# Expert weights in rows of 8 KB: whole gate and up rows into four PSUM banks, down rows in neighbouring pairs

## The chip, the core and the metric

The kernel runs on one core of a Trainium2 chip. The metric is the device time of one execution in microseconds. It is the median of three runs; a separate execution was profiled, and its trace is what the views below show.

## What is computed

The reference is one layer of an encoder with 512 tokens of width 1024: three token mixers (differential attention, attention in a window, attention to 256 memory tokens) whose outputs are gated, summed and projected, then a mixture of 16 experts, then a last norm. The change touches the experts. Each expert picks its 64 best tokens (`cap` below), and every weight is used once, in float32:

```python
def expert_choice_ffn(h, w_router, w_gate, w_up, w_down):
    ...
    cap = max(1, EC_FACTOR * s // N_EXPERTS)
    logits = jnp.einsum('bsd,de->bse', h, w_router).astype(jnp.float32)
    aff = jax.nn.softmax(logits, axis=-1)
    g, idx = lax.top_k(jnp.swapaxes(aff, 1, 2), cap)
    bidx = jnp.arange(b)[:, None, None]
    xe = h[bidx, idx]
    a = jnp.einsum('becd,edf->becf', xe, w_gate)
    u = jnp.einsum('becd,edf->becf', xe, w_up)
    ye = jnp.einsum('becf,efd->becd', jax.nn.silu(a) * u, w_down)
    ye = ye * g[..., None].astype(ye.dtype)
    return jnp.zeros_like(h).at[bidx, idx].add(ye)
```

`w_gate` and `w_up` are 16 matrices of 1024 x 2048, `w_down` 16 of 2048 x 1024, all stored row by row. That is 24 MB for an expert.

## The kernel before

The dense part comes first: norms, projections, the three mixers, the output projection and the router. It takes a little less than half of the span, and its weights come in slabs of 1 MB on SP's queue (lines 85 to 94). The change leaves it alone. Its last lines give, for every token and expert, the affinity (`aff`) and the place among the expert's 64 (`slot`). While its tensor engine is idle, line 610 issues products that nobody reads (`keep_clock`).

The experts run two at a time, eight pairs (line 730). The even expert of a pair has partitions 0 to 63 of its results, the odd one 64 to 127, and the two products of a step lie in different halves of the tensor engine's columns. A pair goes like this:

- `onehots` (line 679) makes 0/1 matrices from the places. `gather` (line 733) multiplies them with the tokens `x2` on the tensor engine (line 738), which picks and transposes the tokens at once; the result is `xT`. `picked_rstd` picks the tokens' norm factors `rp` (line 693).
- Gate and up: for each of four column groups of 512 (`fc`, line 757) there is one PSUM bank for gate and one for up. `half_up` loads two slabs, one for each expert, with four k steps of 128 rows by 512 columns: on each partition four rows of 2 KB (`load_up`, line 698). `mult_up` multiplies them (line 705). Two halves complete a bank.
- After each group ACT makes Silu of the gate bank (line 770), DVE multiplies with up (line 771), the tensor engine transposes the 512 columns in four pieces (line 774), and ACT puts them into `hT` (line 775), the left side of the down product.
- Down: each slab has two blocks of 128 rows of `w_down`, on each partition two rows of 4 KB that lie 128 rows apart (line 784). `down` multiplies into two banks `y` (line 716).
- `scatter` (line 719) copies a bank out of PSUM, multiplies with the transposed affinities (line 723) and adds the result to the tokens' sums `acc` (line 725).

A float32 product appears in the trace as two matmul records, so a k step of both experts into one bank is four of them.

The last pair has a down part of its own (lines 806 to 822): column groups of 512, 256 and 256, whose rows are 2 KB and 1 KB, so that little is left to do when the last weights arrive. The final norm and the output follow.

PSUM has eight banks here: two each named `tr`, `y`, `gate` and `up` (`ps_e`, line 647).

What sets the order of the loads is `slot_e` (line 660). The slabs of the experts go through a fixed list of 1 MB buffers. The first 22 places (`order`) become free one by one in the dense part, and three kinds of buffer among them are used once only: half of `hx`, the two halves of `acc` and `low`. From then on the 18 buffers in `slots` take turns. All loads are issued on SP's queue, which is worked off in order: a load whose buffer is still being read stops the loads behind it. The first four loads that wait for a buffer are issued in halves (line 667), so that each half waits for half of the old slab's products only.

In pair 0 the tensor engine starts on three pairs of slabs in a fixed order (`in_order`) before the second half of the gather is issued (lines 747 to 756). Elsewhere a planner orders the instructions of each engine.

Of the kernel before, what the change touches and what calls it, by code (L numbers as in the profile page):

```python
# [8 lines left out]
F32 = mybir.dt.float32  # L9
# [39 lines left out]
def trunk_kernel(ctx, tc, x, mem, attn_norm_g, mem_norm_g, w_in, w_mem_kv, lq1, lk1, lq2, lk2,  # L49
# [45 lines left out]

# [1 line left out]
    ident = const.tile([P, P], F32, name="ident")  # L97
# [11 lines left out]
    def rstd_of(ss, n, width, tmp):  # L109
        """1 / sqrt(ss / width + EPS), with a Newton step."""  # L110
        s = tmp.tile([P, n], F32, name="rs_s")
        r = tmp.tile([P, n], F32, name="rs_r")
        t = tmp.tile([P, n], F32, name="rs_t")
        u = tmp.tile([P, n], F32, name="rs_u")
        ACT.activation(s, ss, AF.Sqrt, bias=eps, scale=1.0 / width)
        DVE.tensor_scalar(u, ss, -0.5 / width, -0.5 * EPS, op0=OP.mult, op1=OP.add)
        DVE.reciprocal(r, s)
        DVE.tensor_mul(t, r, r)
        DVE.tensor_mul(t, t, u)
        DVE.scalar_tensor_tensor(r, t, 1.5, r, OP.add, OP.mult)  # L120
        return r
# [31 lines left out]
    def proj_n(slab, ah, al, acc, t_outer=False, low=None):  # L153
        """acc[t]: where the tokens of tile t go; two of them may share a bank."""
        nt = len(acc)
        ws = []

        def part(t, k):
            if k // 4 == len(ws):
                ws.append(split_w(slab[:, k // 4 * 4:k // 4 * 4 + 4, :], 4, 256, low))  # L160
            wh, wl = ws[k // 4]
            (o, first, last), a = acc[t], slice(t * P, (t + 1) * P)
            PE.matmul(o, ah[:, k, a], wh[:, k % 4, :], start=(k == 0 and first), stop=False, skip_group_check=True)  # L163
            PE.matmul(o, ah[:, k, a], wl[:, k % 4, :], start=False, stop=False, skip_group_check=True)  # L164
            PE.matmul(o, al[:, k, a], wh[:, k % 4, :], start=False, stop=(k == KT - 1 and last),  # L165
                      skip_group_check=True)

        if t_outer:
            for t in range(nt):
                for k in range(KT):  # L170
                    part(t, k)
                yield t
        else:
            for k in range(KT):
                for t in range(nt):
                    part(t, k)
# [9 lines left out]
    def norm_t(src, nt, g, hi, lo, tmp, gb=None, between=None):  # L186
        """Normalised tokens, transposed and split; the gain on the rows (gb) or on the columns (g)."""
        for t in range(nt):
# [40 lines left out]
    def project(w_o, merged, first=False, spare={}, slabs=range(4)):  # L229
        """spare: a third place for split weights, while two wait for the last heads."""  # L230
        for s in slabs:
# [13 lines left out]

# [1 line left out]
    with ExitStack() as as_:  # L247
# [124 lines left out]

# [1 line left out]
    with ExitStack() as bs:  # L374
# [76 lines left out]

# [1 line left out]
    with ExitStack() as cs:  # L453
# [81 lines left out]

# [1 line left out]
    m_hi = hpool.tile([P, KT, S], F32R, name="m2_hi", tag="h_hi", bufs=1)  # L537
# [55 lines left out]

# [1 line left out]
    aff = ep.tile([P, TT, N_EXP], F32, name="aff")  # L595
# [9 lines left out]
    def keep_clock(n, after, w=512):  # L605
        """Products that nobody reads: an idle tensor engine falls to half its clock."""
        with tc.issue_after(after.ins):
            ps = ps_pj()
            for _ in range(n):
                PE.matmul(ps[:, :w], ident, x2[:, 0, :w], start=True, stop=True)  # L610
# [32 lines left out]

# [1 line left out]
    pse = pool(ctx, "pse", space=PSUM)  # L645
# [6 lines left out]
    hx = hpool.tile([P, 2, 2048], F32, name="hx", tag="h_lo", bufs=1)  # L652
    hT = hx[:, 0].rearrange("p (f c) -> p f c", c=P)
    low, high = (etmp[:, 4 * i:4 * i + 4, :].rearrange("p a b -> p (a b)") for i in range(2))
# [9 lines left out]

    def slab_e(parts, src):
        """A slab of weights; the first ones that wait for a slot come in halves, which are free sooner."""
        n = 1 + (0 <= count[0] - len(order) < 4)
        v = slot_e().rearrange("p (k c) -> p k c", k=parts)
        for i in range(n):
            ks = slice(i * parts // n, (i + 1) * parts // n)  # L670
            nc.sync.dma_start(v[:, ks], src(ks.start, ks.stop - ks.start))
        return v
# [24 lines left out]

    def load_up(w, pr, fc, half):
        return [slab_e(4, lambda k, n, i=i: dap(w, (2 * pr + i) * D * DE + (4 * half + k) * P * DE + fc * 512,
                                                (DE, P), (P * DE, n), (1, 512))) for i in range(2)]  # L700

    def mult_up(sl, half, ps, todo, in_order=False):
        for k4, i in todo:
            k = 4 * half + k4
            mm = PE.matmul(ps[i * 64:(i + 1) * 64], xT[:, k, i * 64:(i + 1) * 64], sl[i][:, k4, :],  # L705
                           start=(k == 0), stop=(k == KT - 1))
            if in_order:
                tc.keep_in_program_order(mm)
        return mm

    def half_up(w, pr, fc, half, ps):
        mult_up(load_up(w, pr, fc, half), half, ps, [(k4, i) for k4 in range(4) for i in range(2)])

# [5 lines left out]
    def scatter(y, ys, n, w, squares=None):  # L719
        (ACT.copy if n else DVE.tensor_copy)(ys[:, :w], y[:, :w])  # L720
        for t in range(TT):
            ps = ps_e(("tr", "tr", "gate", "up")[t] if squares else "tr")[:, :w]
            PE.matmul(ps, gt[:, t * P:(t + 1) * P], ys[:, :w], start=True, stop=True)  # L723
# [6 lines left out]
    for pr in range(N_EXP // 2):  # L730
# [12 lines left out]
        if pr:  # L743
            gather(0)
            gather(4)
            rp = picked_rstd()
        if not pr:
            gather(0, 2)
            gather(2, 2)
            pgs, pus = [ps_e("gate") for _ in range(2)], [ps_e("up") for _ in range(2)]  # L750
            for w, fc, ps in ((w_exp_gate, 0, pgs), (w_exp_up, 0, pus), (w_exp_gate, 1, pgs)):
                mm = mult_up(load_up(w, 0, fc, 0), 0, ps[fc], [(k4, i) for i in range(2) for k4 in range(4)], True)
            behind = mm.ins
            with tc.issue_after(behind):
                gather(4)
                rp = picked_rstd()
        for fc in range(DE // 512):
            if not pr and fc < 2:
                pg, pu = pgs[fc], pus[fc]
            else:  # L760
                pg, pu = ps_e("gate"), ps_e("up")
            with tc.issue_after(behind):
                if pr or fc > 1:
                    half_up(w_exp_gate, pr, fc, 0, pg)
                half_up(w_exp_gate, pr, fc, 1, pg)
                if pr or fc:
                    half_up(w_exp_up, pr, fc, 0, pu)
                half_up(w_exp_up, pr, fc, 1, pu)
            act = ep.tile([P, 512], F32, name="esq", bufs=1)
            silu = ACT.activation(act, pg, AF.Silu, scale=rp)  # L770
            DVE.scalar_tensor_tensor(act, pu, rp, act, OP.mult, OP.mult)  # L771
            ps = ps_e("tr")
            for j in range(4):
                PE.transpose(ps[:, j * P:(j + 1) * P], act[:, j * P:(j + 1) * P], ident)  # L774
            ACT.activation(hT[:, 4 * fc:4 * fc + 4, :], ps.rearrange("p (k c) -> p k c", k=4), AF.Copy)  # L775
# [4 lines left out]

        if pr < N_EXP // 2 - 1:
            y = [ps_e("y") for _ in range(2)]
            for f2 in range(DE // 256):
                sl = [slab_e(2, lambda k, n, i=i: dap(w_exp_down, (2 * pr + i) * DE * D + (2 * f2 + k) * P * D,
                                                      (D, P), (P * D, n), (1, D))) for i in range(2)]
                for j in range(2):
# [5 lines left out]

        # the last norm's gain, from a column to every row
        ones, diag, gf = tmp_a[:, :P], tmp_a[:, 512:1024].rearrange("p (k c) -> p k c", k=4), tmp_a[:, 1024:]
        POOL.memset(ones, 1.0)
        for i, name in enumerate(("gate", "up")):
            ps = ps_e(name)
            DVE.tensor_mul(diag, ident[:, None, :].to_broadcast([P, 4, P]),
# [3 lines left out]

        # the last pair by columns, so that little is left when its last weights arrive
        with tc.issue_after(silu.ins):
# [18 lines left out]

# [1 line left out]
    c1 = 2  # L825
# [59 lines left out]
```

## Time and profile before

| | |
|---|---|
| median of three runs | 1820.2 us (1819.51 to 1820.83) |
| span of the profiled execution | 1817.1 us |
| tensor engine busy | 1706.3 us, 94% |
| mean granted clock of the tensor engine | 0.993 |
| bytes moved by DMA | 477.69 MB |
| HBM read | 468.94 MB, 259 GB/s over the span |

The span reaches from the first to the last instruction of the profiled execution; that and the runs' times are measured apart. "PE" is the tensor engine's matmul, "PEld" its weight load, "SPq" the queue of SP, which issues the loads. In the page's forty slices each digit is a busy share in tenths. "PEclk" is the granted clock. "DMA share" is the mean busy share of the core's 16 DMA engines; it can pass 1 since an engine's packets overlap. Windows give for a stretch the busy time of each engine with its number of instructions, then clock, DMA share and GB/s. The chain is the work that ended last, followed back from the end; a row has start, length, engine and line. KB in a row of DMA issues are 1024 bytes; GB/s count 10^9 bytes.

### The profile page before, as it was taken

The page shows a single profiled execution, that of the slowest core. Times are in us where ns is not written, and L with a number is a line of the kernel's source. Part 1 is how long each engine was busy: PE and PEld are TensorE (multiplying, and loading weights), DVE is VectorE, ACT ScalarE, POOL GpSimd, SP SyncE. Part 2 cuts the span into 40 slices and gives each one's busy share as a digit, 9 for nine tenths or more (in the row PEclk, how much of TensorE's full clock was granted, in tenths as well). Part 3 has the DMA queues.
Part 4 walks back from the last instruction along what each step waited for, and adds up shares of the span by engine and source line. Part 5 has one row for each costly group of instructions (what it writes and reads, how often), then busy time and mean ns, then how long its engine had stood idle before and what let it go on. Part 6 is the DMA issues. An engine that isn't in the chain of part 4 may idle for free.

```text
span 1817.1 us, 21484 instructions
## 1 busy us (share of the span) xinstructions
PE 1706.3 (94%) x8749; PEld 1046.6 (58%) x8749; DVE 523.4 (29%) x1057; ACT 456.0 (25%) x937; POOL 182.1 (10%) x165
## 2 busy tenths in 40 slices
PE   8999999999999999999999988988988988988987
PEld 7888888878879888974343332432422422422423
DVE  4388733464355444441020100100100200101003
ACT  4377752376534343320001000000000000000011
POOL 2043310164430001100000000000000000000000
PEclk9999999999999999999999999999999999999999
DMA  5442222412225226659999999999999999999997
GB/s 167 106 103 71 70 70 93 116 48 70 71 70 186 83 68 244 232 185 333 404 386 394 400 387 398 396 386 402 392 387 406 387 388 405 387 392 401 387 387 258
DMA packets 251557, 477.69 MB, mean 263 GB/s; under 512 B 8257, under 2 KB 84337, under 8 KB 251458
## 3 DMA queue, kind: packets, MB, share of 16 engines
q1 hardware_dynamic: 249506, 470.85, 70.9%
q0 software_dynamic: 1952, 5.47, 1.6%
q8 instruction: 69, 1.13, 0.3%
q14 instruction: 30, 0.25, 0.0%
HBM read 468.94 MB, written 2.10 MB: 259 GB/s over the span
## 4 chain that ended last, share of the span: by engine, by line
PE 73%; DMA 24%; DVE 1%; ACT 1%; SPq 1%; issue 0%; DVEq 0%; ACTq 0%
PE up L705 10%; PE gate L705 9%; PE pj L148 8%; PE pj L150 8%; PE pj L149 8%; DMA slot<-in_w_exp_down_dram 5%; DMA slot<-in_w_exp_up_dram 5%; PE y L716 4%; DMA slab<-in_w_exp_down_dram 4%; PE tr L723 3%; PE tr L738 3%; DMA sp<-in_w_exp_down_dram 2%; DMA etmp<-in_w_exp_down_dram 2%; PE pj L163 2%; PE pj L164 2%; PE pj L165 2%
## 5 line engine op out<-in xcount | busy, mean ns | idle before, releaser
L705 PE MATMUL up<-slot,sp 128*64 128x512 f32 x712 | 201.7, 600 | 23.7 <-DMA slot<-in_w_exp_up_dram 23.7
L716 PE MATMUL y<-slot,hx 128*64 128x512 f32 (+1 forms) x672 | 208.5, 582 | 14.7 <-DMA slot<-in_w_exp_down_dram 14.5
L705 PE MATMUL gate<-slot,sp 128*64 128x512 f32 x680 | 204.0, 597 | 4.8 <-DMA slot<-in_w_exp_gate_dram 4.8
L148 PE MATMUL pj<-h_hi,w 128*128 128x512 f32 x464 | 182.3, 393 | 0.2 <-DVE aks L139 0.2
L150 PE MATMUL pj<-h_hi,w 128*128 128x512 f32 x464 | 182.0, 392 | 0.0
L149 PE MATMUL pj<-h_lo,w 128*128 128x512 f32 x464 | 181.7, 392 | 0.0
L131 DVE TENSOR_TENSOR w<-slab,w 128x1024 fp32r<-128x1024 f32 x111 | 145.1, 1308 | 122.0 <-ACT w L130 121.8
L771 DVE SCALAR_TENSOR_TENSOR esq<-up,rpick,esq 128x512 f32<-128x512 f32 x32 | 24.0, 751 | 511.6 <-PE up L705 503.8
L130 ACT ACTIVATE w<-slab 128x1024 fp32r<-128x1024 f32 x113 | 119.0, 1055 | 119.7 <-PE pj L150 69.8
L705 PEld LDWEIGHTS up<-slot,sp 128*64 128x64 f32 x712 | 63.9, 138 | 116.6 <-issue 91.2
L716 PEld LDWEIGHTS y<-slot,hx 128*64 128x64 f32 x672 | 62.2, 136 | 113.4 <-issue 68.5
L705 PEld LDWEIGHTS gate<-slot,sp 128*64 128x64 f32 x680 | 60.0, 137 | 98.2 <-issue 85.0
L775 ACT ACTIVATE hx<-tr 128x512 f32<-128x512 f32 x32 | 19.1, 597 | 335.1 <-PE tr L774 335.1
L148 PEld LDWEIGHTS pj<-h_hi,w 128*128 128x128 f32 x464 | 87.2, 188 | 18.0 <-PE tr L366 0.4
L150 PEld LDWEIGHTS pj<-h_hi,w 128*128 128x128 f32 x464 | 87.2, 188 | 17.6 <-issue 0.2
L149 PEld LDWEIGHTS pj<-h_lo,w 128*128 128x128 f32 x464 | 87.2, 188 | 16.9
L770 ACT ACTIVATE esq<-gate,rpick 128x512 f32<-128x512 f32 x32 | 22.0, 687 | 286.3 <-PE up L705 179.5
L688 POOL TENSOR_TENSOR sp<-sp,aff 128x512 f32<-128x512 f32 x8 | 8.4, 1048 | 833.8 <-PE tr L778 806.3
L720 DVE COPY etmp<-y 128x512 f32<-128x512 f32 x8 | 5.5, 692 | 273.8 <-PE y L716 273.8
L434 POOL TENSOR_SCALAR bpt<-bpt,bst 128x256 f32<-128x256 f32 (+1 forms) x64 | 72.9, 1156 | 90.2 <-DVE bst L430 54.6
L716 PE MATMUL y<-slab,hx 128*64 128x512 f32 (+1 forms) x208 | 63.6, 569 | 7.2 <-DMA slab<-in_w_exp_down_dram 7.2
L720 ACT COPY etmp<-y 128x512 f32<-128x512 f32 (+1 forms) x9 | 4.8, 538 | 259.6 <-PE y L716 259.6
(326 smaller groups left out, 2969.7 us busy)
## 6 DMA issues: line engine op xcount, KB each, us to landing
slot<-in_w_exp_up_dram SPq DMA_DIRECT2D x87, 1024.0 KB, 14.3
slot<-in_w_exp_gate_dram SPq DMA_DIRECT2D x83, 1024.0 KB, 14.9
slot<-in_w_exp_down_dram SPq DMA_DIRECT2D x75, 1024.0 KB, 18.3
slab<-in_w_in_dram SPq DMA_DIRECT2D x25, 1024.0 KB, 5.2
slab<-in_w_exp_up_dram SPq DMA_DIRECT2D x24, 1024.0 KB, 14.3
slab<-in_w_exp_down_dram SPq DMA_DIRECT2D x21, 1024.0 KB, 18.4
slab<-in_w_exp_gate_dram SPq DMA_DIRECT2D x15, 1024.0 KB, 14.4
hx<-in_w_exp_gate_dram SPq DMA_DIRECT2D x10, 1024.0 KB, 16.1
```

Of the source, the lines that this page charges most:

```text
L130: ACT.activation(wh, v, AF.Copy)
L131: lo = (low or DVE).tensor_sub(wl, v, f32(wh))
L148: PE.matmul(ps, wh[:, k, :], ah[:, k, :], start=(k == 0), stop=False)
L149: PE.matmul(ps, wh[:, k, :], al[:, k, :], start=False, stop=False)
L150: PE.matmul(ps, wl[:, k, :], ah[:, k, :], start=False, stop=(k == KT - 1))
L163: PE.matmul(o, ah[:, k, a], wh[:, k % 4, :], start=(k == 0 and first), stop=False, skip_group_check=True)
L164: PE.matmul(o, ah[:, k, a], wl[:, k % 4, :], start=False, stop=False, skip_group_check=True)
L434: POOL.tensor_scalar(pts[t][:, :n], pts[t][:, :n], st[:, 3, t:t + 1], None, op0=OP.mult)
L705: mm = PE.matmul(ps[i * 64:(i + 1) * 64], xT[:, k, i * 64:(i + 1) * 64], sl[i][:, k4, :], start=(k == 0), stop=(k == KT - 1))
L716: PE.matmul(y[i * 64:(i + 1) * 64, :w], hT[:, f, i * 64:(i + 1) * 64], sl[i][:, j, n:n + w], start=(f == 0), stop=(f == DE // P - 1))
L723: PE.matmul(ps, gt[:, t * P:(t + 1) * P], ys[:, :w], start=True, stop=True)
L738: PE.matmul(ps[:, k4, :], x2[:, t, k * P:(k + 1) * P], oh[:, t, :], start=(t == 0 and k4 == 0), stop=(t == TT - 1 and k4 == n - 1), skip_g ...
```

## The change

Gate and up are no longer worked by column group. A slab is 128 whole rows of one expert's matrix, one row of 8 KB on each partition: one k step for all four column groups. The loop runs over k, then over the four groups, then over the two experts, into four banks `gu0` to `gu3`, one buffer each. All of gate comes first, its Silu goes from the four banks to `hA`, then all of up goes into the same banks. The DVE product, the transposes and the copies to `hT` follow for the four groups.

A down slab still has 256 rows, but partition p now takes rows 2p and 2p+1, one stretch of 8 KB. To fit that, the transposes of all pairs but the last read every second column (`av`). The last pair keeps its column groups and its transposes.

Slabs are no longer loaded in halves. Pair 0 multiplies four k steps of gate (eight slabs) in a fixed order ahead of the second half of the gather, before it was six slabs. Where line 722 and the last norm's gain used the banks `gate` and `up`, they use banks of the name `gu`. The buffer list stays. Comments and docstrings that the diff also drops are left out here.

```diff
-    hT = hx[:, 0].rearrange("p (f c) -> p f c", c=P)
+    hA = hx[:, 0]
+    hT = hA.rearrange("p (f c) -> p f c", c=P)
...
-    def slab_e(parts, src):
-        n = 1 + (0 <= count[0] - len(order) < 4)
-        v = slot_e().rearrange("p (k c) -> p k c", k=parts)
-        for i in range(n):
-            ks = slice(i * parts // n, (i + 1) * parts // n)
-            nc.sync.dma_start(v[:, ks], src(ks.start, ks.stop - ks.start))
+    def slab_e(w, off):
+        v = slot_e()
+        nc.sync.dma_start(v, dap(w, off, (2048, P), (1, 2048)))
         return v
...
-    def load_up(w, pr, fc, half):
-        return [slab_e(4, lambda k, n, i=i: dap(w, (2 * pr + i) * D * DE + (4 * half + k) * P * DE + fc * 512,
-                                                (DE, P), (P * DE, n), (1, 512))) for i in range(2)]
...
+    def gate_up(w, pr, ps, ks, in_order=False):
+        for k in ks:
+            sl = [slab_e(w, (2 * pr + i) * D * DE + k * P * DE) for i in range(2)]
+            for fc in range(DE // 512):
+                for i in range(2):
+                    mm = PE.matmul(ps[fc][i * 64:(i + 1) * 64], xT[:, k, i * 64:(i + 1) * 64],
+                                   sl[i][:, fc * 512:(fc + 1) * 512], start=(k == 0), stop=(k == KT - 1))
+                    if in_order:
+                        tc.keep_in_program_order(mm)
         return mm
...
+    def banks_gu():
+        return [pse.tile([P, 512], F32, name=f"gu{fc}", bufs=1) for fc in range(DE // 512)]
...
-            ps = ps_e(("tr", "tr", "gate", "up")[t] if squares else "tr")[:, :w]
+            ps = (ps_e("tr") if not squares or t < 2 else pse.tile([P, 512], F32, name=f"gu{t}", bufs=1))[:, :w]
...
+        pg = banks_gu()
         if not pr:
             gather(0, 2)
             gather(2, 2)
-            pgs, pus = [ps_e("gate") for _ in range(2)], [ps_e("up") for _ in range(2)]
-            for w, fc, ps in ((w_exp_gate, 0, pgs), (w_exp_up, 0, pus), (w_exp_gate, 1, pgs)):
-                mm = mult_up(load_up(w, 0, fc, 0), 0, ps[fc], [(k4, i) for i in range(2) for k4 in range(4)], True)
-            behind = mm.ins
+            behind = gate_up(w_exp_gate, pr, pg, range(4), True).ins
             with tc.issue_after(behind):
                 gather(4)
                 rp = picked_rstd()
+        with tc.issue_after(behind):
+            gate_up(w_exp_gate, pr, pg, range(0 if pr else 4, KT))
+            for fc in range(DE // 512):
+                silu = ACT.activation(hA[:, fc * 512:(fc + 1) * 512], pg[fc], AF.Silu, scale=rp)
+            pu = banks_gu()
+            gate_up(w_exp_up, pr, pu, range(KT))
+        last = pr == N_EXP // 2 - 1
         for fc in range(DE // 512):
...
-            act = ep.tile([P, 512], F32, name="esq", bufs=1)
-            silu = ACT.activation(act, pg, AF.Silu, scale=rp)
-            DVE.scalar_tensor_tensor(act, pu, rp, act, OP.mult, OP.mult)
+            act = hA[:, fc * 512:(fc + 1) * 512]
+            DVE.scalar_tensor_tensor(act, pu[fc], rp, act, OP.mult, OP.mult)
+            av = act.rearrange("p (b c) -> p b c", c=P) if last else act.rearrange("p (b c j) -> p b j c", b=2, j=2)
             ps = ps_e("tr")
             for j in range(4):
-                PE.transpose(ps[:, j * P:(j + 1) * P], act[:, j * P:(j + 1) * P], ident)
+                PE.transpose(ps[:, j * P:(j + 1) * P], av[:, j] if last else av[:, j // 2, j % 2], ident)
...
-                sl = [slab_e(2, lambda k, n, i=i: dap(w_exp_down, (2 * pr + i) * DE * D + (2 * f2 + k) * P * D,
-                                                      (D, P), (P * D, n), (1, D))) for i in range(2)]
+                sl = [slab_e(w_exp_down, (2 * pr + i) * DE * D + 2 * f2 * P * D).rearrange("p (j c) -> p j c", j=2)
+                      for i in range(2)]
...
-        for i, name in enumerate(("gate", "up")):
-            ps = ps_e(name)
+        for i in range(2):
+            ps = pse.tile([P, 512], F32, name=f"gu{i}", bufs=1)
```

More of the change, by code (lines that the diff above doesn't have):

```diff
@@ L696, in picked_rstd @@
         return r
-    def load_up(w, pr, fc, half):
-        return [slab_e(4, lambda k, n, i=i: dap(w, (2 * pr + i) * D * DE + (4 * half + k) * P * DE + fc * 512,
-                                                (DE, P), (P * DE, n), (1, 512))) for i in range(2)]
[L702 to L708, printed above, removed]
-        return mm
-    def half_up(w, pr, fc, half, ps):
-        mult_up(load_up(w, pr, fc, half), half, ps, [(k4, i) for k4 in range(4) for i in range(2)])
+    def gate_up(w, pr, ps, ks, in_order=False):
[7 more added lines that the diff above has]
+                        tc.keep_in_program_order(mm)
+        return mm
+    def banks_gu():
+        return [pse.tile([P, 512], F32, name=f"gu{fc}", bufs=1) for fc in range(DE // 512)]
     def down(y, f, j, sl, n, w):
@@ L756, in trunk_kernel @@
                 rp = picked_rstd()
-        for fc in range(DE // 512):
[L758 to L768, printed above, removed]
-            act = ep.tile([P, 512], F32, name="esq", bufs=1)
-            silu = ACT.activation(act, pg, AF.Silu, scale=rp)
-            DVE.scalar_tensor_tensor(act, pu, rp, act, OP.mult, OP.mult)
+        with tc.issue_after(behind):
[5 more added lines that the diff above has]
+        last = pr == N_EXP // 2 - 1
+        for fc in range(DE // 512):
+            act = hA[:, fc * 512:(fc + 1) * 512]
+            DVE.scalar_tensor_tensor(act, pu[fc], rp, act, OP.mult, OP.mult)
+            av = act.rearrange("p (b c) -> p b c", c=P) if last else act.rearrange("p (b c j) -> p b j c", b=2, j=2)
             ps = ps_e("tr")
             for j in range(4):
-                PE.transpose(ps[:, j * P:(j + 1) * P], act[:, j * P:(j + 1) * P], ident)
+                PE.transpose(ps[:, j * P:(j + 1) * P], av[:, j] if last else av[:, j // 2, j % 2], ident)
             ACT.activation(hT[:, 4 * fc:4 * fc + 4, :], ps.rearrange("p (k c) -> p k c", k=4), AF.Copy)
@@ L779, in trunk_kernel @@
         ACT.activation(gt, ps, AF.Copy)
-        if pr < N_EXP // 2 - 1:
+        if not last:
             y = [ps_e("y") for _ in range(2)]
             for f2 in range(DE // 256):
-                sl = [slab_e(2, lambda k, n, i=i: dap(w_exp_down, (2 * pr + i) * DE * D + (2 * f2 + k) * P * D,
-                                                      (D, P), (P * D, n), (1, D))) for i in range(2)]
+                sl = [slab_e(w_exp_down, (2 * pr + i) * DE * D + 2 * f2 * P * D).rearrange("p (j c) -> p j c", j=2)
+                      for i in range(2)]
                 for j in range(2):
```

## Prediction

> **What bounds the kernel now.** I read the page first: engines, the forty slices, the packets.
>
> ```profile
> span 1817.1 us, 21484 instructions
> PE 1706.3 (94%) x8749; PEld 1046.6 (58%) x8749; DVE 523.4 (29%) x1057; ACT 456.0 (25%) x937; POOL 182.1 (10%) x165
> ...
> DMA  5442222412225226659999999999999999999997
> ...
> DMA packets 251557, 477.69 MB, mean 263 GB/s; under 512 B 8257, under 2 KB 84337, under 8 KB 251458
> ...
> q1 hardware_dynamic: 249506, 470.85, 70.9%
> ...
> q8 instruction: 69, 1.13, 0.3%
> q14 instruction: 30, 0.25, 0.0%
> ```
>
> PE looks like the bound at 94%, but that is a mean over two stages. The first 18 slices are the dense part, which the change leaves alone. In the other 22, the experts, the DMA engines are full. So the second view is the stretches, cut where the transfers change shape: the start of the experts, their steady part, a stretch that loads only gate and up slabs (2 KB rows), one that loads only down slabs (4 KB rows), and the last pair's narrow columns (1 KB rows).
>
> ```profile
> core 0: us, PE busy (x) PEld busy (x) DVE busy (x) ACT busy (x) POOL busy (x), PEclk, DMA share, GB/s
> 824.00:852.00 28.00, 28.00 (x143) 12.85 (x143) 2.17 (x5) 1.97 (x2) 0.00 (x0) 1.00 0.96 335
> 852.00:1756.00 904.00, 820.80 (x3598) 317.08 (x3594) 81.45 (x126) 48.59 (x78) 7.54 (x8) 0.99 1.04 394
> 1184.00:1236.00 52.00, 46.17 (x196) 15.77 (x194) 2.25 (x3) 3.85 (x6) 0.00 (x0) 0.93 1.05 387
> 1246.00:1280.00 34.00, 30.24 (x116) 10.17 (x114) 0.75 (x1) 1.09 (x2) 1.05 (x1) 1.00 1.03 409
> ...
> 1786.00:1798.00 12.00, 11.55 (x85) 6.97 (x86) 3.59 (x9) 3.85 (x13) 0.00 (x0) 1.00 1.09 346
> ```
>
> From 852 to 1756 us the DMA share is 1.04 of all engines: the transfers set the pace. Full engines deliver 346, 387 and 409 GB/s, and the only thing that changes between them is the length of a row. The third view, the chain, tells whether PE could go faster.
>
> ```profile
> 823.34 4.06 PE gate L705 x13
> ...
> 916.84 1.96 PE tr L723 x4
> ...
> 925.29 7.34 PE tr L738 x64
> ...
> 1168.71 7.34 PE tr L738 x64
> ...
> 1296.59 7.34 PE tr L738 x64
> ```
>
> "tr L738" is the gather that opens a pair of experts. In the steady part a pair takes 1296.59 - 1168.71 = 127.9 us. Pair 0, which found 22 slabs already loaded and hardly waits, goes from 823.34 to the next gather at 925.29 in 102 us, one half gather (some 3.7 us) short of a full pair: PE needs about 106 us for a pair. So PE has 22 us to spare in each.
>
> **The transfers, which carry the sum.** A slab is 1024 KB (1048.6 KB in the units of GB/s). At 346, 387 and 409 GB/s it takes 3.031, 2.710 and 2.564 us. These are 1024, 512 and 256 rows. Halving the rows saved 0.321 us the first time and 0.146 us the second, about half as much: a fixed cost for each row beside a cost for each byte. Whole gate and up rows, and down rows in pairs, make 128 rows of 8 KB. The trace has no such slab (all but 99 of its packets are under 8 KB, and the instructions' queues, 69 + 30, account for those), so I bound it: no further gain, 2.564 us; or the whole remaining row cost of 0.146 us gone, 2.418 us. Half of it, 0.073 us, continues the series and I take that: 2.49 us, 421 GB/s. A loss is not excluded by these rows; it is a rival below.
>
> The Trainium skill (HBM Reference, Specifications) gives about 358 GB/s as the effective share of a core; were that the limit, nothing would be left to win and the time would stay at 1820. The trace disagrees: 409 GB/s in the down stretch, with one core running.
>
> How many slabs does that concern? 904 us at 394 GB/s are 339.7 slabs. Pairs 0 to 6 load 16 down slabs each, 112; the other 227.7 are gate and up. Check: 227.7 x 2.710 + 112 x 2.564 = 904.2 us, the length of the stretch. Afterwards: 339.7 x 2.49 = 845.9 us. **Saved: 58.1 us**, 50.1 of it in gate and up (227.7 x 0.22), 8.3 in down (112 x 0.074). The 22 slabs loaded ahead arrive under the dense part; I give them nothing. The last pair's down loads keep their shapes.
>
> **The start.** Line 665's slabs in halves go, four of them; a slot now comes free only when four products of one k step are done.
>
> ```profile
> 829.18 5.23 SPq L671 DMA_DIRECT2D slot<-in_w_exp_gate_dram  x5
> 835.81 0.37 SPq L671 DMA_DIRECT2D etmp<-in_w_exp_gate_dram  x1
> 843.95 1.76 SPq L671 DMA_DIRECT2D slab<-in_w_exp_down_dram  x2
> ```
>
> At 335 GB/s, the 28 us of the start lose some 4 us against a full stream, partly because SP stands still from 836 to 844 while PE gathers. With the change PE runs eight slabs instead of six ahead of that gather, so eight slots are free for the wait; against that the first refill comes about 1.7 us later, half of a pair of slabs (3.65 us in the row further down). I take 0, between -3 and +2 us.
>
> **PE's order.** A k step of two slabs is still 16 half-products:
>
> ```profile
> 1160.27 1.95 PE L723 MATMUL tr<-etmp 128*128 128x512 f32 x4
> ...
> 1175.98 3.65 PE L705 MATMUL gate<-slot,sp 128*64 128x512 f32 x16
> ...
> 1206.17 0.66 PE L774 MATMUL tr<-ident,esq 128*128 128x128 f32 x4 [0.91 <-DVE esq L771]
> ```
>
> 3.65 us against 2 x 2.49 us of transfer. The four banks hold gate, then up, in one copy, so up's product into a bank waits for its Silu:
>
> ```profile
> L771 DVE SCALAR_TENSOR_TENSOR esq<-up,rpick,esq 128x512 f32<-128x512 f32 x32 | 24.0, 751 | 511.6 <-PE up L705 503.8
> ...
> L775 ACT ACTIVATE hx<-tr 128x512 f32<-128x512 f32 x32 | 19.1, 597 | 335.1 <-PE tr L774 335.1
> ...
> L770 ACT ACTIVATE esq<-gate,rpick 128x512 f32<-128x512 f32 x32 | 22.0, 687 | 286.3 <-PE up L705 179.5
> ```
>
> Bank n is complete a quarter of a step (0.9 us) after bank n-1, and a Silu takes 0.69 us, so bank 0 is read long before up begins and bank 3 has 2.7 us before up reaches it: nothing, and 0.7 us for each Silu if ACT were late. DVE's product and the transposes now come in one bunch at the end of up instead of four times in between. What is exposed is one wait (0.91), one set of transposes (0.66) and one eviction (0.60), 2.2 us, against up to 0.91 us four times now; with 106 against 845.9 / 339.7 x 48 = 119.5 us for a pair this lies under the transfers. The transposes that feed down read every second column; their weight load may be slower, under the same cover.
>
> **Slots.** Eighteen slots turn round in the steady part. PE takes none between its scatter and the first gate products, 15.7 us (1160.27 to 1175.98), and frees the first pair 3.65 us later: 19.4 us, 7.8 slabs at 2.49. At the end of pair 0 (about 917) the stream, running since about 829, has brought 88 / 2.49 = 35 slabs beside the 22, and 48 are used: 9 are waiting. 9 + 7.8 is close to 18, with the next one to be issued ahead. A stall of 0 to 4 us in the first change of pairs; I take **+1**. Later fewer slabs wait, since a pair needs 106 us on PE and 119.5 on DMA.
>
> **The tail.** Before, only the last of four sets of transposes followed the last up slab; now all four may.
>
> ```profile
> 1756.84 1.99 PE up L705 x9
> 1758.83 14.31 DMA slot<-in_w_exp_down_dram
> ...
> 1773.18 7.25 PE y L716 x30
> ...
> 1795.21 6.95 DMA slot<-in_w_exp_down_dram
> ...
> 1802.20 1.09 PE y L716 x6
> ```
>
> Three sets are 2 us of PE at its start; the chain shows PE nearly full from 1773 on but ending on a transfer. Part of the 2 us is absorbed: 0 to +3, I take **+1**.
>
> **Sum.** 1817.1 - 58.1 + 1 + 1 = 1761.0 us of span; the median of the runs is 3.1 us above the profiled span, so **1764.1 us**.
>
> **Rivals.** (1) *Rows over 4 KB bring nothing more*, because the engines cut them into pieces, or a limit near 409 GB/s lies behind the row cost. For it: no row above 4 KB in the trace. Against: 346, 387, 409 still rise by the half-as-much series. Only gate and up gain then: 227.7 x 0.146 = 33.2 us; 1817.1 - 33.2 + 2 + 3.1 = 1789. It is also the way in which the change would not do what it says. The Trainium skill (DMA: Bandwidth & Descriptors, SWDGE vs HWDGE vs iDMA) calls a packet of up to 4096 B preferable; by that rule it would come out this way, and no run here shows it yet.
>
> (2) *PE becomes the bound*: the bunched activations and falls of the clock push a pair beyond 119.5 us.
>
> ```profile
> 1216.00:1220.00 4.00, 1.93 (x4) 0.49 (x6) 0.00 (x0) 0.00 (x0) 0.00 (x0) 0.75 1.05 387
> 1220.00:1224.00 4.00, 4.00 (x12) 1.18 (x10) 0.00 (x0) 0.00 (x0) 0.00 (x0) 0.50 1.04 385
> 1224.00:1228.00 4.00, 4.00 (x20) 1.23 (x18) 0.00 (x0) 0.00 (x0) 0.00 (x0) 0.90 1.05 389
> ```
>
> Such a fall costs PE 1 + 2 + 0.4 = 3.4 us and comes after idling, of which there will be less. It takes 13 us in each pair; with 16 us, six pairs pass 2.5 us over: 1764 + 15 = 1779.
>
> (3) *Slower: 8 KB rows out of one contiguous megabyte are served worse.* Its place is the read side of every gate, up and down slab: all engines then draw on one stretch, where gate and up now draw on four. It decides below 394 GB/s, the mean of now; at the rate of 1 KB rows, 3.031 x 339.7 = 1029.6 us, 126 us longer: 1946. Against it: down slabs draw on only two stretches and are the fastest of all.
>
> (4) *All row cost goes*: 339.7 x 2.418 = 821.4 us, 24.5 us less than forecast: 1740.
>
> **How the numbers follow.** The forecast with its own bounds (slabs of 2.45 to 2.52 us, the three small terms) covers 1750 to 1776: 0.72. Rival 1: 0.12. Rival 2: 0.07. Rival 3: 0.04. Rival 4, beyond 1750: 0.04. No change at all, each saving eaten by a new wait: 0.01. The time is the forecast's, 1764. The forecast alone is under 0.8, so the range reaches to rival 1's 1789: 1750 to 1790. A change under 0.2% (3.6 us) is about what a measurement of this kernel can't tell from none. Rivals 1, 2, 4 and the forecast are all faster by more: 0.95; same 0.01; slower 0.04.
>
> **What would show it.** Packets: one a row, so q1 falls by 256 x 384 + 112 x 128 = 112,640 to about 136,900; if rows are cut at 4 KB, it falls less. The rate in the steady part: 421 GB/s in gate, up and down alike (rival 1: 409, rival 3: under 394). Gather to gather: 119.5 us in the late pairs, with DMA share still over 1 and PE still waiting for transfers; in rival 2 PE waits for DVE or ACT and the DMA share falls. The first change of pairs near 917 us: a dip of a few us. The tail from the last up slab to the end: as before within 3 us. A gain that lies in the dense part, or a steady part that gains without a higher rate, would prove the reasoning wrong.

## The result, and the profile after

The changed kernel takes 1759.41 us (median of four runs, 1758.87 to 1760.45), the kernel before 1819.86 us in the runs beside it. The ratio is 0.9668, with a 95% interval of 0.9655 to 0.9682: faster by 60 us, 3.3%. The forecast was 1764.1, in a range of 1750 to 1790.

The page of the changed kernel, the lines that answer to those of before:

```profile
span 1758.7 us, 21488 instructions
...
PE 1719.1 (98%) x8749; PEld 1079.4 (61%) x8749; DVE 522.9 (30%) x1057; ACT 453.5 (26%) x937; POOL 182.1 (10%) x165
...
DMA  5433222421224326356999999999999999999997
...
DMA packets 138853, 477.69 MB, mean 272 GB/s; under 512 B 8193, under 2 KB 84273, under 8 KB 91650
...
q1 hardware_dynamic: 136802, 470.85, 68.1%
```

The same 470.85 MB go over SP's queue in 136,802 packets instead of 249,506. 112,640 fewer were expected, 112,704 went. The rows were not cut: a packet is a row of 8 KB, and one small packet closes each load on each engine. The 64 beyond the forecast are such small ones, of the four slabs that were issued in two halves before: the packets under 512 B fall from 8257 to 8193. PE is at 98% now, which looks like a new bound; the third experiment shows that it isn't one.

The start and the steady part, as windows of the changed kernel (engine columns as before, the last three are clock, DMA share and GB/s):

```profile
824.00:852.00 28.00, 28.00 (x152) 12.22 (x149) 1.42 (x4) 1.28 (x1) 0.00 (x0) 1.00 0.88 355
852.00:1699.00 847.00, 832.36 (x3580) 348.72 (x3577) 79.54 (x124) 45.06 (x76) 7.54 (x8) 1.00 1.01 420
```

The engines are full from 852 us on, as before, but they deliver 420 GB/s where they delivered 394. The gathers that open the pairs 1, 2, 3 and 7, from the timeline of PE:

```profile
922.69 7.41 PE L735 MATMUL tr<-sp,x 128*128 128x128 f32 x64
...
1029.59 7.41 PE L735 MATMUL tr<-sp,x 128*128 128x128 f32 x64
...
1150.60 7.41 PE L735 MATMUL tr<-sp,x 128*128 128x128 f32 x64
...
1631.42 7.41 PE L735 MATMUL tr<-sp,x 128*128 128x128 f32 x64
```

From pair 2's opening at 1029.59 to pair 7's at 1631.42 are five pairs of 120.4 us on average. The same two openings in the chain of the kernel before:

```profile
1039.91 7.33 PE tr L738 x64
...
1681.94 7.34 PE tr L738 x64
```

There a pair took (1681.94 - 1039.91) / 5 = 128.4 us. The saving is 7.7 to 8.5 us in each of the five pairs; this is a rate, not one stall that went.

The end of the steady part is the arrival of the last up slab, here in the weight loads of PE (the bracket is the wait ahead of it), and the tail after it is in the chain:

```profile
1699.07 0.20 PEld L702 LDWEIGHTS gu<-slot,sp 128*64 128x64 f32 x3 [0.23 <-DMA slot<-in_w_exp_up_dram]
```

```profile
1736.93 7.08 DMA slot<-in_w_exp_down_dram
1744.06 1.09 PE y L713 x6
```

The last up slab is there at 1699.07, before at 1756.84: 57.8 us earlier. From there to the end it takes 59.6 us, before 60.3. So practically all of the gain lies between 824 and 1699 us, and the chain of the tail still goes through a transfer, the 7.08 us above.

### The profile page after: what moved, and what is told of

It is laid out like the page before. It is cut to its first block, busy times and chain, and to the rows that moved or that the text cites. A ratio compares the mean times of both kernels' runs of the same rounds, so it can differ in the third digit from the quotient of the medians.

```text
span 1758.7 us, 21488 instructions
## 1 busy us (share of the span) xinstructions
PE 1719.1 (98%) x8749; PEld 1079.4 (61%) x8749; DVE 522.9 (30%) x1057; ACT 453.5 (26%) x937; POOL 182.1 (10%) x165
## 3 DMA queue, kind: packets, MB, share of 16 engines
q1 hardware_dynamic: 136802, 470.85, 68.1%
## 4 chain that ended last, share of the span: by engine, by line
PE 57%; DMA 40%; ACT 1%; DVE 1%; issue 0%; SPq 0%; DVEq 0%; ACTq 0%
DMA slot<-in_w_exp_up_dram 11%; PE pj L148 8%; PE pj L150 8%; PE pj L149 8%; PE gu L702 7%; DMA slot<-in_w_exp_gate_dram 6%; DMA slab<-in_w_exp_down_dram 5%; DMA slot<-in_w_exp_down_dram 5%; PE y L713 3%; DMA etmp<-in_w_exp_down_dram 2%; DMA sp<-in_w_exp_down_dram 2%; DMA slab<-in_w_exp_gate_dram 2%; DMA sp<-in_w_exp_gate_dram 2%; DMA slab<-in_w_exp_up_dram 2%; PE pj L163 2%; PE pj L164 2%
## 5 line engine op out<-in xcount | busy, mean ns | idle before, releaser
L702 PE MATMUL gu<-slot,sp 128*64 128x512 f32 x1392 | 402.6, 596 | 0.0
L702 PEld LDWEIGHTS gu<-slot,sp 128*64 128x64 f32 x1392 | 136.4, 137 | 218.1 <-issue 208.5
L713 PE MATMUL y<-slot,hx 128*64 128x512 f32 (+1 forms) x672 | 193.9, 579 | 7.4 <-DMA slot<-in_w_exp_down_dram 7.1
L761 DVE SCALAR_TENSOR_TENSOR hx<-gu,rpick,hx 128x512 f32<-128x512 f32 x32 | 23.6, 750 | 462.2 <-PE gu L702 422.3
L755 ACT ACTIVATE hx<-gu,rpick 128x512 f32<-128x512 f32 x32 | 20.1, 685 | 310.3 <-PE gu L702 310.1
L702 PE MATMUL gu<-slab,sp 128*64 128x512 f32 x312 | 98.3, 597 | 0.0
L148 PE MATMUL pj<-o_hi,w 128*128 128x512 f32 x168 | 65.3, 392 | 0.9 <-ACT o_hi L138 0.7
L149 PE MATMUL pj<-o_lo,w 128*128 128x512 f32 x168 | 65.7, 392 | 0.0
L150 PE MATMUL pj<-o_hi,w 128*128 128x512 f32 x168 | 65.1, 391 | 0.4 <-DVE w L131 0.4
## 6 DMA issues: line engine op xcount, KB each, us to landing
slot<-in_w_exp_up_dram SPq DMA_DIRECT2D x89, 1024.0 KB, 19.9
slot<-in_w_exp_gate_dram SPq DMA_DIRECT2D x85, 1024.0 KB, 19.8
slot<-in_w_exp_down_dram SPq DMA_DIRECT2D x75, 1024.0 KB, 19.8
slab<-in_w_exp_down_dram SPq DMA_DIRECT2D x21, 1024.0 KB, 19.8
slab<-in_w_exp_gate_dram SPq DMA_DIRECT2D x20, 1024.0 KB, 19.8
slab<-in_w_exp_up_dram SPq DMA_DIRECT2D x19, 1024.0 KB, 19.8
```

Of the source, the lines that this page charges most:

```text
L148: PE.matmul(ps, wh[:, k, :], ah[:, k, :], start=(k == 0), stop=False)
L149: PE.matmul(ps, wh[:, k, :], al[:, k, :], start=False, stop=False)
L150: PE.matmul(ps, wl[:, k, :], ah[:, k, :], start=False, stop=(k == KT - 1))
L702: mm = PE.matmul(ps[fc][i * 64:(i + 1) * 64], xT[:, k, i * 64:(i + 1) * 64], sl[i][:, fc * 512:(fc + 1) * 512], start=(k == 0), stop=(k == ...
L713: PE.matmul(y[i * 64:(i + 1) * 64, :w], hT[:, f, i * 64:(i + 1) * 64], sl[i][:, j, n:n + w], start=(f == 0), stop=(f == DE // P - 1))
L755: silu = ACT.activation(hA[:, fc * 512:(fc + 1) * 512], pg[fc], AF.Silu, scale=rp)
```

## The experiments

The theory: the steady part is paced by the transfers, and what they take is set by the number of rows, that is the length of a row; the new loop order, the banks and the transposes lie under them. Three others were open: that the gain comes from the new order, that it comes from the contiguous megabyte of a slab, and that PE is by now the bound or nearly so.

**Rows of 4 KB in the new order.** Gate and up take half rows of two k steps, one load for a slab as in the changed kernel; down goes back to its 4 KB rows, and the transposes with it. A slab of half rows holds two of the four column groups only, so gate and up go through k once for each half (`h`).

```diff
+    def slab_w(w, off, pitch, n, c):
+        v = slot_e().rearrange("p (k c) -> p k c", k=n)
+        nc.sync.dma_start(v, dap(w, off, (pitch, P), (P * pitch, n), (1, c)))
+        return v
...
+        n = DE // W                                   # W = 1024
+        for h in range(n):
+            for k0 in ks[::n]:
+                sl = [slab_w(w, (2 * pr + i) * D * DE + k0 * P * DE + h * W, DE, n, W) for i in range(2)]
...
-                sl = [slab_e(w_exp_down, (2 * pr + i) * DE * D + 2 * f2 * P * D).rearrange("p (j c) -> p j c", j=2)
-                      for i in range(2)]
+                sl = [slab_w(w_exp_down, (2 * pr + i) * DE * D + 2 * f2 * P * D, D, 2, D) for i in range(2)]
```

> The changed kernel with its loop order, its four banks and its single loads, but every gate, up and down slab (pairs 0 to 6 for down) in rows of 4 KB: gate and up take 1024 columns of two k steps, down the old 4 KB rows. If the length of a row sets the rate, the steady part runs at 409 GB/s, 2.564 us a slab against 2.489 (421 GB/s) now, 339.7 x 0.075 = 25 us longer than the changed kernel: 1785 us. If the gain came from the new order (all of gate, then all of up, few and large waits), it stays at 1759. If what counts is the contiguous megabyte, gate and up fall back towards 387 GB/s and it takes over 1800.

It took 1789.23 us (ratio to before 0.9833, 0.9819 to 0.9848). A stretch of its steady part, and its loads (the last number is the time from issue to landing):

```profile
1100.00:1130.00 30.00, 27.43 (x106) 9.45 (x103) 1.50 (x2) 1.69 (x3) 1.05 (x1) 1.00 1.03 409
```

```profile
slot<-in_w_exp_up_dram SPq DMA_DIRECT2D x89, 1024.0 KB, 18.5
```

409 GB/s, in gate and up too: the rate that only down had before. Half of the gain is gone again. The time is 4 us above the 1785 expected: 30 us above the changed kernel instead of 25. In the two profiled executions the last up slab comes 27.6 us later (1726.66 against 1699.07 us), some 1 us of that from the start (338 against 355 GB/s between 824 and 852 us), and the tail is as long as there; what the medians differ beyond that is scatter of the executions.

**The old rows in the new order.** The same kernel with W = 512: 2 KB in gate and up, 4 KB in down. A slab then holds one column group, so the groups lie outside the k steps again; all of gate still comes before all of up.

> The same with the old rows: 2 KB in gate and up, 4 KB in down, so that only the order, the banks and the whole loads are new. Row length: rates of 387 and 409 GB/s as before the change, and a time within 4 us of 1820. New order: 1759.

1818.02 us, ratio 0.9993 (0.9983 to 1.0002): no difference from the kernel before. Its steady part against the changed kernel's, the same 300 us of each, this one first:

```profile
1100.00:1400.00 300.00, 268.03 (x1136) 104.64 (x1138) 24.55 (x38) 14.72 (x24) 3.14 (x3) 0.99 1.04 395
```

```profile
1100.00:1400.00 300.00, 291.75 (x1234) 124.98 (x1234) 34.51 (x54) 14.93 (x26) 3.14 (x3) 1.00 1.01 420
```

The mean rate of before is back, and with it the time. The 395 is a mean of two: 386 GB/s from 1170 to 1230 us, where only gate and up arrive, and 409 from 1120 to 1150, where only down does. All of gate first, four banks, the bunched activations, whole loads at the start: together they are worth nothing that these runs can tell, up or down. The rival of the order falls.

**Products in program order.** The planner had, from pair 1 on, put four products of one expert and then four of the other; alone, each leaves half of the columns idle.

```diff
-            gate_up(w_exp_gate, pr, pg, range(0 if pr else 4, KT))
+            gate_up(w_exp_gate, pr, pg, range(0 if pr else 4, KT), True)
...
-            gate_up(w_exp_up, pr, pu, range(KT))
+            gate_up(w_exp_up, pr, pu, range(KT), True)
```

> The changed kernel with the gate and up products of all pairs in program order, so that the two experts' products alternate, where the planner now puts four of one expert and then four of the other. Transfers as the only bound: the late pairs stay at 119.4 to 121 us and the time at 1759, within 2 us. Rival, PE nearly the bound: products of one expert alone take 0.43 us each with half of the columns idle, some 2.5 to 2.6 us a slab against 2.49 us of transfer; then pairs become shorter by 1 us or more each and the time falls to 1752 or below.

1760.19 us, ratio 0.9675 (0.9661 to 0.9689): the same. Three rows show why the order makes no difference. PE at the end of the last up, first in the changed kernel, then (two rows) in this one:

```profile
1692.41 10.30 PE L702 MATMUL gu<-slot,sp 128*64 128x512 f32 x30
```

```profile
1692.93 3.65 PE L702 MATMUL gu<-slot,sp 128*64 128x512 f32 x16 [1.33 <-DMA slot<-in_w_exp_up_dram]
1697.97 3.65 PE L702 MATMUL gu<-slot,sp 128*64 128x512 f32 x14 [1.39 <-DMA slot<-in_w_exp_up_dram]
```

In the one, 30 matmul records (the prediction's half-products, eight for a slab) stretch over 10.3 us and PE counts as busy; in the other a step of 16 takes 3.65 us, and then PE waits 1.4 us for the next slabs. That is the time hidden in the 98%. Both end 3.6 us after their last slab has landed, so both are paced by the transfers. In the changed kernel a slab alone takes 10.3 x 8 / 30 = 2.7 us against 2.49 of transfer, though. Some of that is waiting for its slab, and no run here shows how much: the margin that the planner leaves may be thin.

**Rows spread over the matrix.** The pitch between a slab's rows becomes 64 KB instead of 8 KB. The tokens' columns are multiplied with permuted weight rows here, so the values differ; the work is the same. Down stays as in the changed kernel.

```diff
-            sl = [slab_e(w, (2 * pr + i) * D * DE + k * P * DE) for i in range(2)]
+            sl = [slab_e(w, (2 * pr + i) * D * DE + k * DE, KT * DE) for i in range(2)]
```

> The changed kernel, but each gate and up slab takes its 128 rows of 8 KB at a pitch of 64 KB (every eighth row, spread over the whole matrix) instead of one contiguous megabyte. It multiplies the tokens' columns with permuted weight rows, so its result is another one; the work is the same. Row length alone: 421 GB/s and 1759 us, within 2. If the contiguous megabyte counts, for good or ill, the rate in the gate and up stretches moves by some per cent: 5 GB/s would be 8 us.

1759.70 us, ratio 0.9673 (0.9659 to 0.9688), and the rate:

```profile
1100.00:1400.00 300.00, 291.81 (x1238) 125.10 (x1238) 33.04 (x52) 14.94 (x26) 3.14 (x3) 1.00 1.01 421
```

The same again. Gate and up rows of 8 KB are served alike from one megabyte and from eight. The contiguous slab neither helps nor harms, and with that the slower rival of the prediction has no ground either.

**Each half alone.** First gate and up as changed with down as before:

```diff
-                sl = [slab_e(w_exp_down, (2 * pr + i) * DE * D + 2 * f2 * P * D).rearrange("p (j c) -> p j c", j=2)
-                      for i in range(2)]
+                sl = [slab_w(w_exp_down, (2 * pr + i) * DE * D + 2 * f2 * P * D, D, 2, D) for i in range(2)]
```

> Gate and up as changed, the down slabs of pairs 0 to 6 and the transposes as before the change (rows of 4 KB). If the rows set the pace, 112 slabs take 2.564 us instead of 2.49: 8.3 us longer than the changed kernel, 1768. If the longer down rows bring nothing, 1759.

Then the kernel before with nothing new but down:

```diff
-                sl = [slab_e(2, lambda k, n, i=i: dap(w_exp_down, (2 * pr + i) * DE * D + (2 * f2 + k) * P * D,
-                                                      (D, P), (P * D, n), (1, D))) for i in range(2)]
+                sl = [slot_e().rearrange("p (j c) -> p j c", j=2) for i in range(2)]
+                for i in range(2):
+                    nc.sync.dma_start(sl[i], dap(w_exp_down, (2 * pr + i) * DE * D + 2 * f2 * P * D,
+                                                 (2 * D, P), (D, 2), (1, D)))
```

> The kernel before the change with nothing but the down slabs of pairs 0 to 6 (8 KB rows, transposes of every second column; the first loads that wait for a buffer stay in halves). Rows: 8.3 us less than before, 1811.5. If the part of the gain that belongs to down comes only together with the new order of gate and up, 1820.

Gate and up alone: 1767.34 us, ratio 0.9713 (0.97 to 0.9727), 7.9 us above the changed kernel. Down alone: 1811.53 us, ratio 0.9958 (0.9946 to 0.997), 7.8 us below its own runs of before (1819.32). The steady parts, gate and up first:

```profile
852.00:1640.00 788.00, 770.79 (x3281) 315.42 (x3278) 78.27 (x122) 41.15 (x70) 7.33 (x7) 1.00 1.02 416
```

```profile
852.00:1640.00 788.00, 721.61 (x3174) 283.69 (x3172) 72.19 (x112) 41.98 (x68) 7.33 (x7) 0.99 1.04 397
```

Down is worth the same 8 us with either order of gate and up, and 52 + 8 is the whole: the parts add up, as they should if each row has its price. The second kernel has both lengths of row in one trace. First a stretch in which only down arrives (8 KB), then one with gate and up alone (2 KB):

```profile
1120.00:1150.00 30.00, 27.25 (x104) 9.54 (x104) 0.00 (x0) 1.08 (x2) 1.05 (x1) 1.00 1.01 419
1170.00:1230.00 60.00, 54.43 (x267) 22.39 (x265) 4.39 (x7) 3.85 (x6) 0.00 (x0) 1.00 1.05 387
```

Here gate and up are worked as before the change, and the rate goes with the row alone: 419 where it was 409 GB/s, and 387 as ever.

**The last pair's down too.** What is left with short rows is the last pair's down, 46 us of transfer by the prices of the prediction. Here its first 8 of 16 blocks come as whole rows:

```diff
+        ys = [ps_e("y") for _ in range(2)]
+        for f2 in range(DE // 512 if last else DE // 256):
...
-            y = ps_e("y")
-            for f4 in range(DE // 512):
+            y = ys[1][:, (c - 1) * 256:c * 256] if c else ys[0]
+            for f4 in (2, 3):
```

> The changed kernel, carried into the last pair's down part: the first 8 of its 16 blocks of rows come as whole rows in pairs (8 KB) into both banks, only the last 8 by columns (2 KB and 1 KB). Rows: 8 slabs at 2.49 us instead of 4 at 2.71 and 4 at 3.03, 3.0 us less: 1756.4. If PE sets the pace of the last 55 us (it shows few waits there), nothing is gained: 1759; if the columns' products now bunch behind the last transfers, it gets up to 3 us slower.

1761.94 us, ratio 0.9682 (0.9669 to 0.9695), 2.5 us above the changed kernel; the fastest of its four executions, 1760.55 us, is just above that kernel's slowest, 1760.45. The end of the tail, first the changed kernel, then this one: windows, and PE's last products.

```profile
1740.00:1746.00 6.00, 4.92 (x38) 2.66 (x35) 0.00 (x0) 0.37 (x1) 0.00 (x0) 1.00 0.22 69
```

```profile
1745.59 1.13 PE L720 MATMUL tr<-etmp 128*128 128x256 f32 x4 [0.46 <-ACT etmp L717]
```

```profile
1740.00:1746.00 6.00, 6.00 (x38) 3.21 (x38) 2.61 (x6) 1.96 (x6) 0.00 (x0) 1.00 0.07 21
```

```profile
1747.48 1.13 PE L720 MATMUL tr<-etmp 128*128 128x256 f32 x4 [0.48 <-ACT etmp L717]
```

The transfers end earlier (21 against 69 GB/s in these 6 us), but PE is now full and its last products start 1.9 us later: the first 8 blocks, in whole rows, bring no column group nearer to its end than the others, so the three groups finish closer together and the scatters (the busy DVE and ACT of the second window) bunch behind the last weights. The last of the outcomes expected came. Here the length of a row is not all that a load's shape decides.

**Less work for PE in the tail.** If PE were all that sets the tail, taking 2 us of it away should show. The last norm's gain (two products) is spread ahead of the last pair's gate instead of after its up; in a second kernel the products are in program order as well.

```diff
+        if pr == N_EXP // 2 - 1:
+            ones, diag = ep.tile([P, 256], F32, name="esq", bufs=1)[:, :P], etmp[:, 3, :]
...
+                ps = ps_e("tr")
...
+                PE.matmul(ps, ones, diag.rearrange("p k c -> p (k c)"), start=True, stop=True)
...
+        pg = banks_gu()
```

> The changed kernel with the last norm's gain (two products, 2 us of PE) spread to all rows ahead of the last pair's gate, under the transfers, instead of after its up. If PE sets the pace of the tail, as the slower version with whole rows in the last pair suggests, the 2 us leave the tail: 1757.5. If transfers set it, nothing moves: 1759.4.

> The same, and the gate and up products of all pairs in program order, which in its own run ended the last up 1.1 us sooner (1701.55 against 1702.65). PE-bound tail: 2 + 1 us less than the changed kernel, 1756.5. Transfers: 1759.4.

1759.47 us (0.9673, 0.9659 to 0.9686) and 1760.19 us (0.9673, 0.966 to 0.9686): nothing moved. The profiled spans are 1757.5 both times, 1.2 us under the changed kernel's, less than its runs scatter. What PE waited in the tail, between 1697 and 1746 us, in the changed kernel and then in the first of the two (us in all, times, longest):

```profile
PE y L713 <- DMA slot<-in_w_exp_down_dram: 0.6, 1, 0.6
PE tr L720 <- ACT etmp L717: 0.5, 1, 0.5
PE tr L766 <- ACT hx L767: 0.3, 1, 0.3
PE y L713 <- DMA slab<-in_w_exp_down_dram: 0.2, 1, 0.2
```

```profile
PE y L713 <- DMA slot<-in_w_exp_down_dram: 1.8, 2, 1.6
PE tr L720 <- ACT etmp L717: 0.9, 2, 0.5
PE tr L720 <- DVE etmp L717: 0.7, 1, 0.7
PE tr L777 <- ACT hx L778: 0.2, 1, 0.2
```

The waits grew from 1.6 to 3.6 us: the 2 us came back, as waits for transfers and for the copies out of PSUM. In the tail PE and the transfers are nearly balanced: less work for PE alone ends at the other side. No version tried here is faster than the changed kernel.

## Why the prediction was right

**The transfers.** Predicted: 421 GB/s, 2.49 us a slab, 58.1 us. Measured: 420 to 421 GB/s, and the last up slab 57.8 us earlier, of which the start has 1.3. So the slabs gave some 56.4 us. The step that carried it was an extrapolation, that each halving of rows saves half as much as the one before. It held: 0.321, 0.146 and now 0.075 us a slab, and the kernels with 2, 4 and 8 KB rows run at 387, 409 and 420 GB/s whatever the order of the work around them. The packet records of the traces show the price directly: one packet takes 88 ns at 2 KB, 164 at 4 KB and 313 at 8 KB (medians), so twice the bytes take 12 to 15 ns less than twice the time. The split came out too: 8.3 us were put on down, 7.8 and 7.9 measured.

**The small terms.** The start was put at 0 and gained 1.3 us: 355 against 335 GB/s in 28 us are 0.56 MB. The slot stall in the first change of pairs was put at 1 us; the eight-microsecond windows around 917 us show 420, 423 and 417 GB/s, no stall. SP did wait for PE there, up to 8.3 us for one slot, but eight loads were in flight, 20 us of work, and they carried the stream over the gap. The tail was put at +1 and came at -0.6. So the small terms came out 4.0 us better than forecast and the slabs 1.7 us worse, which makes the 2.3 us between the predicted span of 1761.0 and the measured 1758.7; that they offset each other is luck. The other 2.4 us of the miss lie in the 3.1 us between span and median, which is no constant: after the change it is 0.7, in the experiments 0.4 to 2.8. Every execution after the change and in the experiments took 1.7 to 1.9 us longer than its own span; the rest depends on which execution was profiled. One profiled execution does not fix terms of this size.

**PE.** Predicted: 106 us for a pair, under the transfers. With the products in order the first unhindered pair takes from 922.72 to 1028.25, 105.5 us. What the prediction had not seen is that the planner would reorder the products; it filled most of the margin of 13 us in a pair (PE is busy for 116.5 to 118.7 us of each) without costing anything.

**The rivals.** A limit at 4 KB: refuted, 421 against 409. The Trainium skill (DMA: Bandwidth & Descriptors, SWDGE vs HWDGE vs iDMA) prefers packets of at most 4096 B, in a table on the descriptors that GpSimd writes; for these loads, which SP issues, the trace shows no such preference, rows of 8 KB were faster by 3%. PE as the bound: refuted by the program order. The contiguous megabyte: refuted by the spread rows. All row cost gone: refuted, the rate stops at 421. From 4 KB to 8 KB a slab went from 2.564 to 2.489 us, with 8 rows fewer on each of 16 engines: 9.4 ns for a row. The prediction's two steps give 10.0 and 9.1 ns, so the price of a row hardly changes with its length, and by an estimate from it the 128 rows that are left still cost 0.07 to 0.08 us a slab; no run has longer rows.

The prediction took 358 GB/s as a possible limit of one core and found the trace against it. That section of the Trainium skill (HBM Reference, Specifications) means a core whose neighbour streams too, and puts a core alone near 425 GB/s; the 420 measured here agree with that, and the figure was no rival.

Pairs take 119.4 and 121.0 us in turn. Before the change they alternated too, 127.9 and 128.8, and the rate is the same in both kinds, 420 to 421 GB/s now, so no transfer time is lost in the longer ones. The chain has one link of 21.4 instead of 19.8 us among the up loads of each longer pair. The cause was not traced.

## What to carry to other kernels

Where the DMA engines are full, look at the rate by row length before anything else: stretches with different rows in the same trace give the price of a row, and with it the gain of longer ones, here to within 3% (56.4 of 58.1 us). Ask of every other part of such a change only whether it stays under the transfers, and test that by putting the old rows into the new order. And stop at the tail: where what is left after the last transfer matters, the shape of the loads decides the order of the work, and longer rows can cost more than they save, here 2.5 us.

## What was not expected

Loads with fewer rows pass SP's queue differently. One row of SP's waits in the changed kernel (us in all, times, longest), and one of its loads, with the time to landing:

```profile
SPq L669 <- DMA slot<-in_w_exp_up_dram: 147.9, 70, 3.6
```

```profile
slot<-in_w_exp_up_dram SPq DMA_DIRECT2D x89, 1024.0 KB, 19.9
```

A slab lands 19.9 us after its issue, eight times 2.49 us: in the steady part SP waits for an older load to land, not for a free slot, and eight are in flight. What sets the eight was not traced. With 4 KB rows it was 18.5 us, 7.2 slabs; with the old 2 KB rows 14.3 us, 5.3 slabs. There the issue itself holds SP, in the kernel before (shortest, median and longest in ns):

```profile
L671 SPq DMA_DIRECT2D slot<-in_w_exp_up_dram x91: 367/2534/2858, 680.7 to 1742.4; - x91
```

The median is 2.53 us for 2 KB rows, 2.31 for 4 KB and 0.33 for 8 KB, but the shortest is 0.37 us at 2 and at 4 KB too, so the rest is most likely waiting for room in the queue. This bears on a rival that had no run of its own: that with short rows the issue on SP, 2.53 us beside 2.71 us a slab, sets the pace. Five slabs under way at once and a DMA share of 1.05 speak against it.

The transposes that read every second column load their weights in 209 ns, before 140 ns (medians). At 112 of them, all but the last pair's, this is 8 us of PE's weight loads, all under the transfers.
